# A two-layer hybrid trunk on one core: partition changes in four transfers instead of sixteen, keys ahead of queries, small steps spread out

## The chip, the cores and the metric

The kernel runs on one core of a Trainium2 chip. The metric is the device time of one execution in microseconds (us), lower is better. TensorE (PE in the profile) multiplies matrices, VectorE (DVE) and ScalarE (ACT) work on tiles, GpSimd (POOL) does small work and issues transfers, SyncE (SP) issues transfers.

## The reference

A sequence of 256 tokens of width 2048 goes through two layers. Each projects the normalised input once and gives the columns to three mixers, whose gated outputs are merged and added to x:

```python
def hybrid_layer(x, ...):
    h = rms_norm(x, norm_g)
    (c_q, c_kv, k_rope, z_a, u_b, v_b, z_b, q_c, k_c, v_c, a_r, z_c, gate_logits) = split(h @ w_in)
    y_a = mla_branch(c_q, c_kv, k_rope, ...) * silu(z_a)
    y_b = sgu_branch(gelu(u_b), gelu(v_b), ...) * silu(z_b)
    y_c = gla_branch(q_c, k_c, v_c, a_r, ...) * silu(z_c)
    g = sigmoid(gate_logits)
    merged = sum(g[b] * (y[b] @ w_branch[b]) for b in range(3))
    return x + merged @ w_out

def mla_branch(c_q, c_kv, k_rope, ...):          # 8 heads, 128 plain + 64 rotary
    q = rms_norm(c_q) @ w_uq
    k_nope, v = rms_norm(c_kv) @ w_ukv
    q, k = rms_norm(q), rms_norm(concat(k_nope, k_rope))   # per head; then the rotary part is turned
    return causal_block_attention(q, k, v)       # blocks of 128 queries
```

The sgu mixer multiplies by a 128 x 128 position matrix per group; the gla mixer is a gated linear attention with a decay from a_r, in chunks of 128.

## The kernel before

**Products.** All is float32. Each operand of a big product is split in a high part and a rest (`whi`, `wlo` of the weights; two halves of `xT`, `cT`, `mT`, `yT`), and three products of 128 x 512 make one. `Weights.chunk` loads 512 KB of weights (`wraw`, 4 buffers, queue SP), ACT copies `whi` (L65) and DVE subtracts `wlo` (L66), 3 buffers each. `block` (L194) goes over the chunks; a chunk is 12 products on PE (L207 to L209: two slices of the contraction, two token tiles, three products). So 24 products are a block of 4 slices, as those on `cT` are. The tokens' side has to stand with its features on the partitions.

**Small work.** Everything else is handed out in steps. After every three products `block` calls `step()`, which draws one step from the first generator in the list `work`; `pause(n)` lets n steps pass. `finish()` draws what is left. The framework's scheduler then sets each engine's order, with the weight splits ahead, and puts in the waits. Engines run their instructions in that order, so whoever stands behind a wait waits too.

**Changing partitions.** `move` (L269) brings features to the partitions: DVE transposes blocks of 32 x 32 into `part` (L275), and 16 transfers of 32 KB, in runs of 128 bytes, carry `part` to its place (L282). `move_split` (L284) moves into `whole` and splits that in two with ACT (L229) and DVE (L230). For the last groups (`mT3`, and `xT2`, `xT3` of the next layer) `transpose_split` (L246) has PE transpose with the identity (L242, tile `ptr`) instead.

**A layer**, in the order of PE: the two low-rank inputs `cq` (moved to `cT`, queue POOL), a narrow block of 96 columns (`accT`: the shared rotary key `krT`, the decay's input `arT`), the gate `sza`, then seven blocks on `cT`: queries (three: two plain, one rotary), keys (two, `kn`), values (two). The decay's products `pk` and `pz` (`decay`, L410) come 44 steps after they are put on the list. Queries and keys go through squares, sums and `r_q`, `r_k` on POOL (L126), rotation on DVE, and `move`: `qTn`, `qTr`, `kTz`, `kTn`. Meanwhile PE goes on with the `qc` block; the scores (`psc`, L561 and L563), the transposed probabilities (`ppt`) and the values (`ppv`) are drawn between its products. Then the gla mixer (`plv`, factors `X`, `AT`), the sgu mixer, the merge (`mT`) and the output (`xT`).

Of the kernel before, what the change touches and what calls it, by code (L numbers as in the profile page):

```python
# [71 lines left out]
def trunk(ctx: ExitStack, tc: tile.TileContext, a, out):  # L72
# [49 lines left out]
    def rsqrt(ss, n, inv, name):  # L122
        m = ts(f"m_{name}")
        V.tensor_scalar(m[:, :n], ss, inv, EPS, ALU.mult, ALU.add)
# [51 lines left out]
    work, pending = [], set()  # L176
# [13 lines left out]
    def finish():  # L190
        while work:
            step()
# [44 lines left out]
    def transpose2(src, b):  # L237

        p = pB("ptr")
        for k in range(2):  # L240
            for t in range(NT):
                nc.tensor.transpose(p[:, k * S + t * P:k * S + (t + 1) * P],  # L242
                                    src[:, t, (b + k) * P:(b + k + 1) * P], ident)
        return p

    def transpose_split(src, scale, name):  # L246

        dst = t8(name, F32R)
        pending.add(id(dst))
        dv = dst.rearrange("p (h k s) -> p h (k s)", h=2, k=4)  # L250

        def steps():
            yield from pause(4)
            ps = [transpose2(src, kk) for kk in (0, 2)]
            for kk, p in zip((0, 2), ps):
                if callable(scale):
                    for k in range(2):
                        c = slice((kk + k) * S, (kk + k + 1) * S)
                        split(dv[:, 0, c], dv[:, 1, c], p[:, k * S:(k + 1) * S], scale(kk + k))
                else:  # L260
                    c = slice(kk * S, (kk + 2) * S)
                    split(dv[:, 0, c], dv[:, 1, c], p, scale)
            pending.discard(id(dst))
            yield

        work.append(steps())
        return dst

    def move(dst, src, queue=nc.sync):  # L269

        part = t4("part")
        for t in range(NT):
            V.transpose(part.rearrange("p (k t c) -> p k t c", k=4, t=NT)[:, :, t, :],  # L275
                        src[:, t, :].rearrange("p (k c) -> p k c", k=4))
        pv = part.rearrange("p (n i b) -> p n i b", n=8, i=4)
        dst = dst if isinstance(dst, list) else [dst, dst]
        dv = [d.rearrange("p (n j b) -> p n j b", n=8, j=4) for d in dst]
        for j in range(4):  # L280
            for i in range(4):
                queue.dma_start(dv[i // 2][32 * i:32 * i + 32, :, j, :], pv[32 * j:32 * j + 32, :, i, :])  # L282

    def move_split(src, scale, name, queue=nc.sync, wait=0):  # L284

        dst, whole = t8(name, F32R), t4("whole")
        dv = dst.rearrange("p (h n) -> p h n", h=2)
# [3 lines left out]
        def steps():  # L291
            yield from pause(wait)
            if callable(scale):
                for k in range(4):
                    c = slice(k * S, (k + 1) * S)
                    split(dv[:, 0, c], dv[:, 1, c], whole[:, c], scale(k))
            else:
                split(dv[:, 0], dv[:, 1], whole, scale)
            pending.discard(id(dst))
            yield  # L300

        if wait:
            work.append(steps())
        else:
            list(steps())
# [40 lines left out]
    for l in range(DEPTH):  # L346
# [63 lines left out]
        def decay():  # L410
# [9 lines left out]
            for t in range(NT):  # L420
# [8 lines left out]
                V.scalar_tensor_tensor(la[:, t, :], z, 0.0, e, ALU.min, ALU.subtract)  # L429
# [22 lines left out]
        def rotate(dst, tmp, src, j, shape):  # L452
# [3 lines left out]
            V.tensor_tensor(dst, src, bc(TA, 0, 64), ALU.mult)  # L456
            V.tensor_tensor(tmp[:, :, :, 0:32], src[:, :, :, 32:64], bc(TB, 0, 32), ALU.mult)
            V.tensor_tensor(tmp[:, :, :, 32:64], src[:, :, :, 0:32], bc(TB, 32, 32), ALU.mult)
            V.tensor_tensor(dst, dst, tmp, ALU.add)

        def squares(dst, src):

            for t in range(NT):
                sq = t4("sq")[:, 0:src.shape[2]]
                act(sq, src[:, t, :], AF.Square)
                V.tensor_reduce(dst[:, t * 8:(t + 1) * 8], sq.rearrange("p (h d) -> p h d", h=NH), AX.X, ALU.add)

        qkg = ts("qkg", 1)
        V.tensor_tensor(qkg, gain(l, 24), gain(l, 25), ALU.mult)
        qn = t8("qn").rearrange("p (t c) -> p t c", t=NT)  # L470
        qr = t4("qr").rearrange("p (t c) -> p t c", t=NT)
        qTn = t8("qTn")
        for j in range(3):
            acc = block(lq, 4)
            for t in range(NT):
                dst = qn[:, t, j * 512:(j + 1) * 512] if j < 2 else qr[:, t, :]
                act(dst, acc[t], AF.Copy, scale=rc[:, t:t + 1])
        ssq = ts("ssq", 32)
        squares(ssq[:, 0:16], qn)
        squares(ssq[:, 16:32], qr)  # L480
        V.tensor_tensor(ssq[:, 0:16], ssq[:, 0:16], ssq[:, 16:32], ALU.add)
        rq = rsqrt(ssq[:, 0:16], 16, 1.0 / 192, "q")
        rqs = ts("rqs")
        V.tensor_scalar(rqs, rq, SCALE, None, ALU.mult)
        qrr, qrt = t4("qrr"), t4("qrt")
        rotate(v4(qrr), v4(qrt), qr.rearrange("p t (h d) -> p t h d", h=NH), 0, NH)
        qTr = t4("qTr")

        def half(dst, src, j):
            move(dst[:, j * 1024:(j + 1) * 1024], src[:, :, j * 512:(j + 1) * 512], nc.gpsimd)  # L490

        def move_queries():
            half(qTn, qn, 0)
            yield from pause(14)
            move(qTr, qrr.rearrange("p (t c) -> p t c", t=NT), nc.gpsimd)
            yield from pause(14)

        work.append(move_queries())
# [4 lines left out]
        kn = t8("kn").rearrange("p (t c) -> p t c", t=NT)  # L503
        for j in range(2):
            acc = block(lk, 4)
            for t in range(NT):
                act(kn[:, t, j * 512:(j + 1) * 512], acc[t], AF.Copy, scale=rc[:, 2 + t:3 + t])
        ssk = ts("ssk")
        squares(ssk[:, 0:16], kn)
        for t in range(NT):  # L510
            V.tensor_scalar(ssk[:, t * 8:(t + 1) * 8], ssk[:, t * 8:(t + 1) * 8], sskr[:, t:t + 1], None, ALU.add)
        rk = rsqrt(ssk[:, 0:16], 16, 1.0 / 192, "k")
        rk4 = rk.rearrange("p (t h) -> p t h", t=NT)
        krs = t4("krs")
        V.tensor_tensor(v4(krs), v1(krr).broadcast_to([P, NT, NH, 64]),
                        rk4.unsqueeze(3).broadcast_to([P, NT, NH, 64]), ALU.mult)
# [6 lines left out]
        kf = kn.rearrange("p t (h d) -> p (t h) d", h=NH)  # L523
        V.tensor_tensor(kf, kf, rk.unsqueeze(2).broadcast_to([P, 16, P]), ALU.mult)
        kTn = t8("kTn")

        def move_keys():
            move(kTz, krs.rearrange("p (t c) -> p t c", t=NT), nc.gpsimd)
            yield from pause(14)
            half(kTn, kn, 0)  # L530
            yield from pause(14)
            half(qTn, qn, 1)
            yield from pause(14)
# [429 lines left out]
```

## Time and profile before

| | us |
|---|---|
| median of three runs | 1860.86 |
| lowest and highest | 1855.51, 1862.33 |
| the profiled execution, own time | 1858.54 |
| its span | 1856.8 |
| PE busy in it | 1832.8 (99%) |
| DVE, ACT, POOL busy | 1131.2, 918.5, 188.1 |

The profiled execution is one that the hardware profiler recorded; its span is the time from its first to its last instruction, 1.7 us shorter than its own time. A product's start is exact, while its end is modelled, so a row's duration overlaps the next row's. All times of the prediction are set against 1858.54.

### The profile page before, as it was taken

The page shows a single profiled execution, that of the slowest core. Times are in us where ns is not written, and L with a number is a line of the kernel's source. Part 1 is how long each engine was busy: PE and PEld are TensorE (multiplying, and loading weights), DVE is VectorE, ACT ScalarE, POOL GpSimd, SP SyncE. Part 2 cuts the span into 40 slices and gives each one's busy share as a digit, 9 for nine tenths or more (in the row PEclk, how much of TensorE's full clock was granted, in tenths as well). Part 3 has the DMA queues.
Part 4 walks back from the last instruction along what each step waited for, and adds up shares of the span by engine and source line. Part 5 has one row for each costly group of instructions (what it writes and reads, how often), then busy time and mean ns, then how long its engine had stood idle before and what let it go on. Part 6 is the DMA issues. An engine that isn't in the chain of part 4 may idle for free.

```text
span 1856.8 us, 22945 instructions
## 1 busy us (share of the span) xinstructions
PE 1832.8 (99%) x8312; PEld 1518.6 (82%) x8312; DVE 1131.2 (61%) x1450; ACT 918.5 (49%) x1124; POOL 188.1 (10%) x301
## 2 busy tenths in 40 slices
PE   8999999999999999999999999999999999999999
PEld 7877888888888888888888778888888888888887
DVE  6766657876455655555566656578664556454554
ACT  6764445564444344444456635455544444444443
POOL 2217500000000000000022274000000000000000
PEclk9999999999999999999999999999999999999999
DMA  9657775475566665666866588754755766656754
GB/s 318 219 182 207 185 223 182 144 213 185 193 208 201 204 205 193 206 203 217 255 210 195 190 204 189 219 182 151 212 182 193 211 200 205 205 192 208 239 198 158
DMA packets 211026, 375.24 MB, mean 202 GB/s; under 512 B 119776, under 2 KB 120448, under 8 KB 210400
## 3 DMA queue, kind: packets, MB, share of 16 engines
q1 hardware_dynamic: 198624, 352.60, 60.3%
q0 software_dynamic: 10848, 18.78, 3.9%
q10 hardware_dynamic: 1440, 2.39, 0.4%
q8 instruction: 65, 1.06, 0.2%
q14 instruction: 49, 0.40, 0.1%
HBM read 348.52 MB, written 4.19 MB: 190 GB/s over the span
## 4 chain that ended last, share of the span: by engine, by line
PE 78%; DMA 2%; DVE 1%; POOL 1%; issue 1%; ACT 0%; SPq 0%; DVEq 0%; ACTq 0%; POOLq 0%
PE acc L209 25%; PE acc L207 25%; PE acc L208 25%; PE plv L706 1%; DMA kTn<-part 1%; DMA kTz<-part 1%; PE po L729 0%; PE pmx L803 0%; DVE wlo L66 0%; DMA qTn<-part 0%; DMA qTr<-part 0%; PE psc L563 0%; PE ppv L594 0%; PE psc L561 0%; DMA whole<-part 0%
## 5 line engine op out<-in xcount | busy, mean ns | idle before, releaser
L66 DVE TENSOR_TENSOR wlo<-wraw,whi 128x1024 fp32r<-128x1024 f32 (+1 forms) x642 | 781.1, 1218 | 634.0 <-ACT whi L65 632.8
L65 ACT ACTIVATE whi<-wraw 128x1024 fp32r<-128x1024 f32 (+1 forms) x642 | 677.3, 1056 | 792.9 <-PE acc L209 745.2
L207 PE MATMUL acc<-whi,xT 128*128 128x512 f32 x1792 | 703.1, 393 | 8.7 <-ACT whi L65 8.7
L208 PE MATMUL acc<-wlo,xT 128*128 128x512 f32 x1792 | 701.1, 391 | 5.2 <-DVE wlo L66 5.2
L209 PE MATMUL acc<-whi,xT 128*128 128x512 f32 x1792 | 700.6, 391 | 0.0
L207 PEld LDWEIGHTS acc<-whi,xT 128*128 128x128 f32 x1792 | 337.8, 189 | 78.5 <-ACT whi L65 9.5
L208 PEld LDWEIGHTS acc<-wlo,xT 128*128 128x128 f32 x1792 | 338.0, 189 | 75.8 <-DVE wlo L66 6.9
L209 PEld LDWEIGHTS acc<-whi,xT 128*128 128x128 f32 x1792 | 337.9, 189 | 70.0
L207 PE MATMUL acc<-whi,mT 128*128 128x512 f32 x256 | 99.9, 390 | 0.0
L209 PE MATMUL acc<-whi,mT 128*128 128x512 f32 x256 | 99.8, 390 | 0.0
L208 PE MATMUL acc<-wlo,mT 128*128 128x512 f32 x256 | 99.6, 389 | 0.0
L209 PEld LDWEIGHTS acc<-whi,mT 128*128 128x128 f32 x256 | 48.1, 188 | 9.9
L207 PEld LDWEIGHTS acc<-whi,mT 128*128 128x128 f32 x256 | 48.1, 188 | 9.9
L208 PEld LDWEIGHTS acc<-wlo,mT 128*128 128x128 f32 x256 | 48.1, 188 | 9.9
L207 PE MATMUL acc<-whi,yTa 128*128 128x512 f32 x128 | 49.8, 389 | 0.0
L208 PE MATMUL acc<-wlo,yTa 128*128 128x512 f32 x128 | 49.8, 389 | 0.0
L209 PE MATMUL acc<-whi,yTa 128*128 128x512 f32 x128 | 49.8, 389 | 0.0
L207 PE MATMUL acc<-whi,yTb 128*128 128x512 f32 x128 | 49.8, 389 | 0.0
L208 PE MATMUL acc<-wlo,yTb 128*128 128x512 f32 x128 | 49.8, 389 | 0.0
L209 PE MATMUL acc<-whi,yTb 128*128 128x512 f32 x128 | 49.8, 389 | 0.0
L207 PE MATMUL acc<-whi,yTc 128*128 128x512 f32 x128 | 49.8, 389 | 0.0
L208 PE MATMUL acc<-wlo,yTc 128*128 128x512 f32 x128 | 49.8, 389 | 0.0
(235 smaller groups left out, 1551.9 us busy)
## 6 DMA issues: line engine op xcount, KB each, us to landing
wraw<-in_w_big SPq DMA_DIRECT2D x634, 512.0 KB, 4.3
whole<-part SPq DMA_DIRECT2D x320, 32.0 KB, 4.2
x<-x POOLq DMA_DIRECT2D x8, 512.0 KB, 4.7
x<-in_x SPq DMA_DIRECT2D x2, 1024.0 KB, 8.9
whole<-part POOLq DMA_DIRECT2D x64, 32.0 KB, 4.1
qTn<-part POOLq DMA_DIRECT2D x64, 32.0 KB, 4.8
kTn<-part POOLq DMA_DIRECT2D x64, 32.0 KB, 5.2
qkT<-part SPq DMA_DIRECT2D x64, 32.0 KB, 4.1
```

The costliest lines, as they stand in the source:

```text
L65: nc.scalar.activation(hi[:, c], raw[:, c], AF.Copy)
L66: nc.vector.tensor_tensor(lo[:, c], raw[:, c], hi[:, c].bitcast(F32), ALU.subtract)
L207: nc.tensor.matmul(o, xh[:, c], wh, start=kt + k == 0, stop=False)
L208: nc.tensor.matmul(o, xh[:, c], wl, start=False, stop=False)
L209: nc.tensor.matmul(o, xl[:, c], wh, start=False, stop=kt + k == kts - 1)
L706: nc.tensor.matmul(p[:, h * P:(h + 1) * P], X[:, 0, h, :], X[:, 1, h, :], start=True, stop=True)
```

## The change

1. `move` orders `part` otherwise: the transposes read every fourth column (16 bytes apart) and 4 transfers of 128 KB, in runs of 1 KB, carry it (8 of 64 KB for `kTz`, which has two halves). What lands is in the order "j n b" and `natural` reads it back in order: in ACT's and DVE's splits, in an added copy by ACT (`qTn`, `qTr`, `qkT`), or directly in the score products.
2. The splits are cut in 4 or 8 pieces and come by a timer, `after(n, f)`, n steps later, instead of at once or from the list.
3. `transpose_split` is gone: `mT3`, `xT2`, `xT3` use `move_split` with a wait of 12 steps. The decay's generator so comes earlier, as the splits of `cT` don't stand ahead of it on the list.
4. Keys are projected ahead of queries (also in the weights' order, `_lay_out`); their movement is one generator, each query half has its own, and the rotation and the squares are spread over steps. The factor SCALE is put into `r_q`'s power.

```diff
 def rsqrt(ss, n, inv, name, times=1.0):
...
+    def after(n, f):
+        timers.append((clock[0] + n, f))
     def step():
+        clock[0] += 1
+        for t in [t for t in timers if t[0] <= clock[0]]:
+            timers.remove(t)
+            t[1]()
...
-    def transpose2(src, b):
...
-    def transpose_split(src, scale, name):
...
+    def natural(d):
+        return d.rearrange("p (j n b) -> p n j b", j=4, n=8)
     def move(dst, src, queue=nc.sync):
         part = t4("part")
         for t in range(NT):
-            V.transpose(part.rearrange("p (k t c) -> p k t c", k=4, t=NT)[:, :, t, :],
-                        src[:, t, :].rearrange("p (k c) -> p k c", k=4))
...
-        for j in range(4):
-            for i in range(4):
-                queue.dma_start(dv[i // 2][32 * i:32 * i + 32, :, j, :], pv[32 * j:32 * j + 32, :, i, :])
+            V.transpose(part.rearrange("p (i k t b) -> p t k i b", i=4, k=4, t=NT)[:, t],
+                        src[:, t, :].rearrange("p (k b i) -> p k i b", k=4, i=4))
+        dst = dst if isinstance(dst, list) else [dst]
+        for j in range(4):
+            o = slice(j * 256, (j + 1) * 256)
+            pv = part[32 * j:32 * j + 32, :].rearrange("p (i n) -> p i n", i=4)
+            for k, d in enumerate(dst):
+                r = slice(64 * k, 64 * k + 64) if len(dst) == 2 else slice(0, 128)
+                queue.dma_start(d[r, o], pv[16 * k:16 * k + 16] if len(dst) == 2 else pv)
     def move_split(src, scale, name, queue=nc.sync, wait=0):
...
+        def parts():
             if callable(scale):
+                for n in range(8):
+                    split(dv[:, 0, n], dv[:, 1, n], wv[:, n], scale(n // 2))
             else:
+                for j in range(4):
+                    split(dv[:, 0, :, j], dv[:, 1, :, j], wv[:, :, j], scale)
             pending.discard(id(dst))
+        after(wait, parts)
...
+        def keys():
+            yield from pause(4)
+            krs = rotary_keys()
+            yield from pause(1)
             move(kTz, krs.rearrange("p (t c) -> p t c", t=NT), nc.gpsimd)
+            for j in range(2):
+                yield from pause(4)
+                kf = heads(kn, j).rearrange("p t (h d) -> p t h d", h=4)
+                V.tensor_tensor(kf, kf, th(rk, j).unsqueeze(3).broadcast_to([P, NT, 4, P]), ALU.mult)
+                yield
+                move(half(kTn, j), heads(kn, j), nc.gpsimd)
+        work.append(keys())
+        def move_queries(j):
+            yield from pause(4)
+            whole = t4("whole")
+            move(whole, heads(qn, j), nc.gpsimd)
+            after(14, lambda: act(pieces(half(qTn, j)), natural(whole), AF.Copy, scale=qkg))
...
+        def rotary_queries():
+            yield from pause(2)
+            qrr, qrt = t4("qrr"), t4("qrt")
+            yield from rotate_steps(v4(qrr), v4(qrt), qr.rearrange("p t (h d) -> p t h d", h=NH), 0, NH)
+            whole = t4("whole")
+            move(whole, qrr.rearrange("p (t c) -> p t c", t=NT), nc.gpsimd)
             yield from pause(14)
+            act(pieces(qTr), natural(whole), AF.Copy)
+            yield from pause(2)
...
-        mT.append(transpose_split(merge_block(3), 0.5, "mT3"))
+        mT.append(move_split(merge_block(3), 0.5, "mT3", wait=12))
...
-                turn = move_split if nb < 2 else transpose_split
-                xT.append(turn(x, lambda k, l=l, nb=nb: gain(l + 1, 4 * nb + k), f"xT{nb}"))
+                xT.append(move_split(x, lambda k, l=l, nb=nb: gain(l + 1, 4 * nb + k), f"xT{nb}", wait=12))
```

**ACT behind the narrow block of layer 0.** Before, `arT` is copied, the weights' splits go on, and the splits of the second low-rank input (`cT_523`) and the decay's key (`kr`, from the tile `pk`) come later:

```order
L399 ACTIVATE arT<-accT 32x256 x2
L65 ACTIVATE whi<-wraw 128x1024 x4
L229 ACTIVATE cT_523<-whole,first_in 128x256 x2
L404 ACTIVATE wa<-wa_raw 96x512
L65 ACTIVATE whi<-wraw 128x1024
L229 ACTIVATE cT_523<-whole,first_in 128x256 x2
L65 ACTIVATE whi<-wraw 128x1024 x2
L440 ACT_TABLE_LOAD
L440 ACTIVATE th<-acc_659,rs 128x512
L65 ACTIVATE whi<-wraw 128x1024
L440 ACTIVATE th<-acc_660,rs 128x512
L417 ACTIVATE junk,sskr<-pk,r_x 128x64
```

After (`cT_511` is that second input):

```order
L376 ACTIVATE arT<-accT 32x256 x2
L237 ACTIVATE cT_511<-whole,first_in 128x128 x4
L65 ACTIVATE whi<-wraw 128x1024
L237 ACTIVATE cT_511<-whole,first_in 128x128 x4
L381 ACTIVATE wa<-wa_raw 96x512
L65 ACTIVATE whi<-wraw 128x1024
L394 ACTIVATE junk,sskr<-pk,r_x 128x64
L395 ACTIVATE kr<-pk,r_x 128x64
L237 ACTIVATE cT_502<-whole,first_in 128x128 x2
L394 ACTIVATE junk,sskr<-pk,r_x 128x64
```

The splits of `cT_511` moved ahead of four weight splits, and `pk`'s readers ahead of the gate's `th`.

**PE at the first scores of layer 0.** Before, one of the scores' groups is followed by eight products of the `qc` block (`acc`):

```order
L563 MATMUL psc<-kTn,qTn 128x128
L208 MATMUL acc_1840<-wlo,xT_94 128x512
L209 MATMUL acc_1840<-whi,xT_94 128x512
L207 MATMUL acc_1839<-whi,xT_94 128x512
L208 MATMUL acc_1839<-wlo,xT_94 128x512
L209 MATMUL acc_1839<-whi,xT_94 128x512
L207 MATMUL acc_1840<-whi,xT_94 128x512
L208 MATMUL acc_1840<-wlo,xT_94 128x512
L209 MATMUL acc_1840<-whi,xT_94 128x512
L584 MATMUL ppt<-c_ident,smx 128x128
```

After:

```order
L552 MATMUL psc<-kTn,qTn 128x128
L216 MATMUL acc_1405<-wlo,xT_96 128x512
L217 MATMUL acc_1405<-whi,xT_96 128x512
L215 MATMUL acc_1404<-whi,xT_97 128x512
L574 MATMUL ppt<-c_ident,smx 128x128
L550 MATMUL psc<-kTz_1106,qTr 128x256
L574 MATMUL ppt<-c_ident,smx 128x128
L552 MATMUL psc<-kTn,qTn 128x256
```

Three products stand there now. The scores themselves moved later in the block (slices `xT_96` where it was `xT_94`).

**POOL in layer 0 from the query's reciprocal root on.** Before, `r_k` stands behind the 32 transfers of `qTn` and `qTr`:

```order
L126 TENSOR_TENSOR r_q<-m_q,neghalf 128x16
L282 DMA qTn<-part 32x8x32 x16
L282 DMA qTr<-part 32x8x32 x16
L126 TENSOR_TENSOR r_k<-m_k,neghalf 128x16
L521 MEMSET kTz_1298 64x1024
L522 MEMSET kTz_1299 64x1024
```

After, the keys' end, the queries' and the rotary queries' transfers (the three `whole`):

```order
L263 DMA kTz_1107<-part 64x1x256
L263 DMA kTn<-part 128x1x256 x8
L263 DMA whole<-part 128x1x256 x8
L126 TENSOR_TENSOR r_q<-m_q,neghalf 128x16
L263 DMA whole<-part 128x1x256 x4
```

`r_k` moved ahead of all of these (and of eight transfers of `kTz`), and `r_q` to just ahead of the rotary queries.

## Rows read from the trace of the kernel before

**Rows 1.** The profile's first part: busy time, share of the span and instructions of each engine:

```profile
PE 1832.8 (99%) x8312; PEld 1518.6 (82%) x8312; DVE 1131.2 (61%) x1450; ACT 918.5 (49%) x1124; POOL 188.1 (10%) x301
```

**Rows 2.** The waits of PE: line, what it waited for, time in total, times, longest, in us (longest row):

```profile
PE acc L207 <- ACT whi L65: 8.7, 3, 5.6
```

**Rows 3.** Timeline of PE in layer 0, 131 to 199 us: start, duration, engine, line, operation, output<-inputs, and in brackets the idle time ahead of it with what ended it:

```profile
131.63 0.50 PE L207 MATMUL acc<-whi,cT 128*128 128x512 f32 x1 [1.72 <-ACT kn L507]
...
156.17 0.49 PE L207 MATMUL acc<-whi,xT 128*128 128x512 f32 x1 [2.48 <-ACT whi L65]
157.43 0.50 PE L208 MATMUL acc<-wlo,xT 128*128 128x512 f32 x1 [0.77 <-DVE wlo L66]
...
158.56 0.63 PE L209 MATMUL acc<-whi,xT 128*128 128x512 f32 x1
...
161.12 0.63 PE L209 MATMUL acc<-whi,xT 128*128 128x512 f32 x1
...
167.95 0.50 PE L208 MATMUL acc<-wlo,xT 128*128 128x512 f32 x1 [0.46 <-DVE wlo L66]
...
198.35 0.35 PE L563 MATMUL psc<-kTn,qTn 128*128 128x128 f32 x1 [1.68 <-issue]
```

**Rows 4.** The same timeline of PE in layer 1, 1054 to 1122 us:

```profile
1054.92 0.50 PE L207 MATMUL acc<-whi,cT 128*128 128x512 f32 x1 [1.72 <-ACT kn L507]
...
1077.63 0.51 PE L207 MATMUL acc<-whi,xT 128*128 128x512 f32 x1 [0.65 <-ACT whi L65]
1078.89 0.51 PE L208 MATMUL acc<-wlo,xT 128*128 128x512 f32 x1 [0.76 <-DVE wlo L66]
...
1090.53 0.79 PE L208 MATMUL acc<-wlo,xT 128*128 128x512 f32 x1 [3.18 <-DVE wlo L66]
...
1121.15 0.46 PE L563 MATMUL psc<-kTn,qTn 128*128 128x128 f32 x2 [0.51 <-DMA kTn<-part]
```

**Rows 5.** Timelines of ACT and of POOL in layer 0, the row of each at 154 and 160 us:

```profile
154.02 1.15 ACT L538 ACTIVATE qTn<-qTn,qkg 128x1024 f32<-128x1024 f32 x1 [7.07 <-DMA qTr<-part]
...
160.37 2.94 POOL L126 TENSOR_TENSOR r_k<-m_k,neghalf 128x16 f32<-128x16 f32 x1
```

**Rows 6.** Timeline of PE where eight transposes of x stand, and two products behind them:

```profile
911.52 1.04 PE L242 MATMUL ptr<-c_ident,x 128*128 128x128 f32 x8
912.32 0.47 PE L207 MATMUL acc<-whi,mT 128*128 128x512 f32 x1
912.63 0.39 PE L208 MATMUL acc<-wlo,mT 128*128 128x512 f32 x1
```

**Rows 7.** Timeline of PE at the first products behind the narrow block, in layer 0 (two) and in layer 1:

```profile
57.65 0.40 PE L207 MATMUL acc<-whi,xT 128*128 128x512 f32 x1
57.88 0.40 PE L208 MATMUL acc<-wlo,xT 128*128 128x512 f32 x1
...
980.94 0.40 PE L207 MATMUL acc<-whi,xT 128*128 128x512 f32 x1
```

**Rows 8.** Timeline of POOL in layer 0 at 57 us and in layer 1 at 980 us:

```profile
57.48 1.04 POOL L126 TENSOR_TENSOR r_c<-m_c,neghalf 128x4 f32<-128x4 f32 x1 [9.39 <-DVE m_c L124]
58.48 8.11 POOL L282 DMA_DIRECT2D whole<-part  x14
...
979.54 6.38 POOL L282 DMA_DIRECT2D whole<-part  x11
```

**Rows 9.** The profile's part on DMA issues: output<-input, issuing engine, count, KB of each, median us from issue to landing:

```profile
wraw<-in_w_big SPq DMA_DIRECT2D x634, 512.0 KB, 4.3
...
whole<-part POOLq DMA_DIRECT2D x64, 32.0 KB, 4.1
...
kTn<-part POOLq DMA_DIRECT2D x64, 32.0 KB, 5.2
...
rope_g<-in_rope_g ACTq DMA_DIRECT2D x1, 128.0 KB, 2.8
```

**Rows 10.** Instructions grouped by line and shape: count | busy us, mean ns of one | idle time of the engine ahead of them:

```profile
L66 DVE TENSOR_TENSOR wlo<-wraw,whi 128x1024 fp32r<-128x1024 f32 x634 | 774.5, 1223 | 631.6 <-ACT whi L65 630.5
L65 ACT ACTIVATE whi<-wraw 128x1024 fp32r<-128x1024 f32 x634 | 671.4, 1060 | 788.9 <-PE acc L209 741.6 <-issue 28.4 <-DVE wlo L66 5.0
...
L574 ACT ACTIVATE smx<-smx,nbias,rqs 128x128 f32<-128x128 f32 x16 | 7.7, 482 | 10.9 <-DVE nbias L572 10.9
...
L229 ACT ACTIVATE cT<-whole,first_in 128x256 fp32r<-128x256 f32 x16 | 7.2, 500 | 3.5 <-DMA whole<-part 2.2 <-DMA ba<-in_b_a 1.3
...
L126 POOL TENSOR_TENSOR r_k<-m_k,neghalf 128x16 f32<-128x16 f32 x2 | 5.9, 2934 | 0.0
...
L538 ACT ACTIVATE qTn<-qTn,qkg 128x1024 f32<-128x1024 f32 x4 | 4.6, 1144 | 12.3 <-DMA qTr<-part 7.1 <-DMA qTn<-part 5.2
...
L275 DVE STREAM_TRANSPOSE part<-qrr 128x512 f32<-128x512 f32 x4 | 2.5, 666 | 0.0
...
L418 ACT ACTIVATE kr<-pk,r_x 128x64 f32<-128x64 f32 x4 | 1.2, 304 | 0.0
```

**Rows 11.** Timeline of DVE in the gated linear attention of layer 0: one step of the factors and the masked copies of two levels:

```profile
331.27 0.44 DVE L715 COPY_PREDICATED AT<-c_lvl,plv 128x256 f32<-128x256 int32 x1
...
352.56 0.42 DVE L694 TENSOR_TENSOR X<-X,qkT 128x256 f32<-128x256 f32 x1
352.89 1.31 DVE L715 COPY_PREDICATED AT<-c_lvl,plv 128x256 f32<-128x256 int32 x2
```

More of the change, by code (lines that the diff above doesn't have):

```diff
@@ L190, in finish @@
     def finish():
-        while work:
+        while work or timers:
             step()
@@ new lines, in trunk @@
+        rotate(v1(krr), v1(krt), v1(kr), 1, 1)
+        kn = t8("kn").rearrange("p (t c) -> p t c", t=NT)
+        ssk = ts("ssk")
+        for j in range(2):
+            acc = block(lk, 4)
+            for t in range(NT):
+                act(heads(kn, j)[:, t], acc[t], AF.Copy, scale=rc[:, 2 + t:3 + t])
+            squares(th(ssk[:, 0:16], j), heads(kn, j), 4)
+        for t in range(NT):
+            V.tensor_scalar(ssk[:, t * 8:(t + 1) * 8], ssk[:, t * 8:(t + 1) * 8], sskr[:, t:t + 1], None, ALU.add)
@@ L470, in trunk @@
+        rk = rsqrt(ssk[:, 0:16], 16, 1.0 / 192, "k")
+        kTz = [t4("kTz0"), t4("kTz1")]
+        nc.gpsimd.memset(kTz[0][64:128, :], 0.0)
+        nc.gpsimd.memset(kTz[1][0:64, :], 0.0)
+        kTn = t8("kTn")
         qn = t8("qn").rearrange("p (t c) -> p t c", t=NT)
         qr = t4("qr").rearrange("p (t c) -> p t c", t=NT)
-        qTn = t8("qTn")
+        qTn, qTr = t8("qTn"), t4("qTr")
+        pieces = lambda v: v.rearrange("p (n j b) -> p n j b", n=8, j=4)
+        half = lambda v, j: v[:, j * 1024:(j + 1) * 1024]
@@ L486, in trunk @@
[L486 to L493, printed above, removed]
-            yield from pause(14)
-            move(qTr, qrr.rearrange("p (t c) -> p t c", t=NT), nc.gpsimd)
-            yield from pause(14)
-        work.append(move_queries())
-        krr, krt = ts("krr", 128, 1), ts("krt", 128, 1)
@@ L502, in trunk @@
-        rotate(v1(krr), v1(krt), v1(kr), 1, 1)
[L503 to L511, printed above, removed]
@@ L525, in trunk @@
[L525 to L533, printed above, removed]
-            half(kTn, kn, 1)
-            yield from pause(14)
-            for j in range(2):
-                c = slice(j * 1024, (j + 1) * 1024)
-                act(qTn[:, c], qTn[:, c], AF.Copy, scale=qkg)
-            yield from pause(4)
@@ L634, in trunk @@
         for j in range(2):
-            move(qkT[:, j], qk[:, j])
+            whole = t4("whole")
+            move(whole, qk[:, j])
+            after(14, lambda j=j, w=whole: act(pieces(qkT[:, j]), natural(w), AF.Copy))
         vc = t8("vc").rearrange("p (t c) -> p t c", t=NT)
@@ L643, in trunk @@
         finish()
-        yT = {0: [move_split(ya[:, :, j * 512:(j + 1) * 512], 0.5, f"yTa{j}") for j in range(2)]}
+        yT = {0: [move_split(ya[:, :, j * 512:(j + 1) * 512], 0.5, f"yTa{j}", wait=14) for j in range(2)]}
         AT = t4("AT")
@@ L843, in trunk @@
         finish()
-        yT[1] = [move_split(uz[:, :, j * 512:(j + 1) * 512], 1.0, f"yTb{j}") for j in range(2)]
+        yT[1] = [move_split(uz[:, :, j * 512:(j + 1) * 512], 1.0, f"yTb{j}", wait=14) for j in range(2)]
         gate_block(1)
         for nb in range(2):
-            mT.append(move_split(merge_block(nb), 0.5, f"mT{nb}"))
+            mT.append(move_split(merge_block(nb), 0.5, f"mT{nb}", wait=14))
         gate_block(2)
```

116 lines of the change are left out of this document (42 added, 74 removed).

## The prediction

> **What bounds the kernel now.** The profile's first part comes first: PE is busy for 1832.8 of 1856.8 us [rows 1], so only 24 us are idle, and what isn't idle is product after product at a fixed spacing: behind the narrow block they start 0.23 us apart [rows 7], 24 of them (one block on `cT`) in 5.44 us. The time can fall in two ways, by fewer PE instructions or by fewer waits of PE. So the waits of PE come next: most are for the weights' split on ACT [rows 2]. That doesn't make ACT the limit; the timeline of PE shows where these waits lie: nearly all in the attention, between the blocks on `cT` and the first scores, once in each layer [rows 3, 4].
>
> In layer 0 the idle times there are 1.72, 2.48, 0.77, 0.46 and 1.68 us, 7.1 together; each hides 0.16 more, as a row's modelled 0.39 is longer than the spacing of 0.23: 7.9. Behind the wait at 156 us seven products run 0.43 apart ((161.12 - 158.56)/6) instead of 0.23, another 1.4 [rows 3]. Layer 1 has 1.72, 0.65, 0.76, 3.18 and 0.51, 6.8, with the hidden part 7.6, and I take as long a slow stretch behind its longest wait, 1.4 [rows 4]. Together 18.3 us.
>
> The cause is a queue. ACT sat 7.07 us at the copy of `qTn`, for transfers of `qTr`, with weights' splits queued behind it; and POOL reached `r_k` only at 160.37 us, behind all the queries' transfers, so the keys came late too [rows 5]. A transfer costs POOL 8.11/14 = 0.58 us to issue, and a move has 16, thus 9.3 us [rows 8].
>
> **The change, part by part.**
>
> *Transposes on PE go.* There are 32. Eight hold the products up from 911.52 to 912.63 less one spacing, 0.88 us [rows 6]; four times that is 3.5 us off PE for certain. In their place `mT3`, `xT2` and `xT3` take four DVE transposes (0.67 each [rows 10]), four issues, a landing and pieces of splits: some 12 us. PE comes to that slice after 12 slices of 6 products, 16.3 us. It holds, but on DVE and ACT the splits stand between weights' splits, which leaves by the order as little as 0.4 us. I cost it at nothing.
>
> *The old waits go.* With four transfers a move takes POOL 2.3 us instead of 9.3, `r_k` stands ahead of all of these, and the copy of `qTn` no longer waits behind the rotary queries. The 18.3 us go, if nothing takes their place. Three things do.
>
> *How long a move takes to land (L).* No row shows a transfer of 128 KB from SBUF to SBUF in runs of 1 KB. The nearest are `rope_g`, 128 KB in 1-KB runs, 2.8 us, and the old moves, 4.1 to 5.2, which are as long as a weight load of 512 KB, 4.3 [rows 9]. The bounds are 2.8 and 5.2; I take 3.4, nearer the row of the same size and runs, as that one ran on another queue. The page "DMA: Bandwidth & Descriptors" of the Trainium skill (section "Why small descriptors are slow (HBM only)") says that transfers within SBUF don't suffer from small runs; by that rule 1-KB runs land no sooner than 128-byte runs did, and the sum would be that of the first rival.
>
> *New wait at the decay.* `pk` comes 15 products behind the narrow block, its second half 17 further on, and that waits for ACT's `kr`. ACT now has the splits of `cT_511` ahead of it, and these wait for the move. Layer 0: `r_c` ends at 58.5, four issues end at 60.8 [rows 8], landed at 60.8 + L. Then ACT does eight quarter splits (between 0.30 and 0.50 each, started some 0.1 closer: 0.28, 2.2 together), two weights' splits (2.1), `wa` and the readers of `pk` (about 1.2): 5.5 us [rows 10]. So 66.3 + L, with L = 3.4 at 69.7. PE is there at 57.65 + 32 x 0.227 and a little, 65.2 [rows 7]: it waits 4.5 us. Behind that wait are weights' splits too, so PE has nothing else. Layer 1: POOL is free at 979.5, landed at 981.9 + L, ACT done at 990.8; PE, from 980.94, comes at 988.3: 2.5 us. Together 7.0, and a slow stretch behind the longer wait, 1.4. At L = 2.8 it is 5.8, at 5.2 it is 10.6, with the stretch besides.
>
> *New wait ahead of the scores.* Times from the first product on `cT`. Keys end at 10.9, their `r_k` (2.93 [rows 10]) at about 16.5, the rotary keys are turned and moved from about 22; then eight issues for `kTz`, eight for `kTn`, eight for `whole` of the queries: the last issue at about 39.5, with DVE's transposes between (an estimate from 0.58 an issue and 0.67 a transpose). DVE's rotation of `qr` needs a buffer that this move frees, 39.5 + L; its rest, four transposes and two or three weights' subtractions (1.22 each) and four issues take 9.1, another L, and the added copy to `qTr` 1.14 like `qTn`'s [rows 10]: 49.7 + 2L = 56.5. PE comes to the first score after 168 products on `cT` and 70 of `qc`, 54.0, with half a us of small waits 54.5. It waits 2.0 us in each layer, 4.0 in all. At L = 2.8 it is 1.6, at 5.2 it is 11.2 in all.
>
> *Fewer products between scores.* Eight scores, then three products (0.7 us) to the first `ppt`; before there were eight (1.8 us). From score to `ppt` lie the masked maxima on DVE and the exponent on ACT (0.48 [rows 10]), 1.5 to 2 us; later groups have `ppt` and `ppv` without any products. Upper bound 3.2 us a layer; lower bound nothing, as smaller waits stand there now. I take 2.0, in two layers 4.0.
>
> *What costs nothing.* SP issues 4 instead of 16 transfers a move; no PE wait lies there. Three copies of 1.14 on ACT a layer, hidden: ACT is 49% busy [rows 1]. The products between the levels of the gla mixer are spread otherwise (15 each); DVE's eight factor steps of 0.42 and two masked copies a level [rows 11] run ahead of that by a few us, by the order, so at most 1 us is lost or won. The transposes read every fourth column. Rows bound what that can do: the factor step 352.56, at a level that reads in scattered short runs, takes 0.42 as at every level, while the masked copies take 1.31/2 = 0.65 there and 0.44 at a coarser level [rows 11]. So between nothing and half as much again (0.3 us each); I take nothing, as the transpose has one input like the factor step rather than the copy's three.
>
> *Sum.* -18.3 - 3.5 + 7.0 + 1.4 + 4.0 + 4.0 = -5.4. From the profiled execution's 1858.5 (2.3 below the median of the three) that gives **1853**. L = 2.8 gives 1849.5, L = 4.2 gives 1858.
>
> **The rivals.**
>
> *1. Moves land as slowly as now.* L = 4.2 to 5.2. For it: the old moves land with the weight loads, 4.1 to 5.2 against 4.3, as if they queued together [rows 9]. Against it: fewer and larger pieces, and `rope_g`. At 5.2: -21.8 + 10.6 + 1.4 + 11.2 + 4.0 = +5.4. 1858 to 1864.
>
> *2. The new waits are covered.* L near 2.8 or below, pauses that overlap what I laid end to end, and scores that cost no more than now. What stays is the decay's wait in layer 0, 4 us: 1858.5 - 21.8 + 4 = 1841. For it: a chain laid out by hand is an upper bound wherever a DVE or ACT step can slip ahead. Against it: in layer 0 `pk` waits for a chain that nothing can shorten.
>
> *3. The strided transposes are slow.* This ends slower. If each takes twice its 0.67, a move takes 2.7 us longer. The second half of `cT` has it in its chain in both layers (5.4), the rotary queries too (5.4), the two `mT3` and `xT3` have little slack (2 to 2.5 each, 7 in all); 18 us: 1871, with some hidden 1868. Each 0.1 us of a transpose is worth 2.6; from 0.2 on the change gives nothing, from 0.55 on it is slower by 0.5%. Against it: the factor step's 0.42; for it: the masked copy's 0.65 [rows 11]. The page "SBUF — State Buffer" of the Trainium skill (its note on cachelines, section "Door 1") says that lines are of 16 bytes and each step to a new line costs; by that rule every element of these transposes, 16 bytes apart, would pay. The masked copy agrees, the factor step doesn't.
>
> **How the numbers follow.** A difference under 0.5%, 9.3 us, can't be told from none here. My forecast 0.38, rival 1 0.13, rival 2 0.34, rival 3 0.15. Faster than 1849.2: rival 2 and 0.06 of the forecast, 0.40. Slower: 0.12 of rival 3 and 0.03 of rival 1, 0.15. The rest, 0.45, is the same. The likeliest's own range is 1849 to 1858; with the others 1839 to 1866, which leaves out part of rivals 2 and 3, under 0.2.
>
> **What the profile after would show.** No `ptr` on PE and 32 instructions fewer. The waits of PE at `acc` for ACT's `kn` gone; no ACT idle of 7 us at `qTn`. A PE idle of 3 to 6 us within 10 us behind the narrow block of layer 0, ended by ACT (`kr` or a weights' split), about half in layer 1. The first score waits 1 to 3 us for the `qTr` copy. The moves' landing between 2.8 and 4.2 in the DMA part, and the transposes at 0.67 still. It is wrong if transposes take 0.9 or more, if the landing is outside, or if waits appear in the gla mixer or at `mT3`.

## The result and the profile after

The changed kernel takes 1880.8 us (median; 1879.2 to 1881.4) against 1861.3 of the kernel before: a ratio of 1.011, 95% interval 1.0088 to 1.0132. The forecast was 1853, with a range up to 1866. It is 20 us slower, where I had it 5 faster.

The page's first part, to compare with [rows 1]:

```profile
PE 1837.6 (98%) x8280; PEld 1519.7 (81%) x8280; DVE 1179.2 (63%) x1560; ACT 938.8 (50%) x1232; POOL 81.7 (4%) x117
```

PE has 32 instructions fewer (8280 for 8312), and the span is 1879.1 instead of 1856.8 us: of the 22.3 us more, 17.5 are idle PE (41.5 us instead of 24.0) and the rest is busy time that runs slowly. POOL fell from 188 to 82 us, and DVE rose by 48.

The waits of PE (engine, line, what it waited for, us in total, times, longest; [rows 2] has the longest row of before):

```profile
PE psc L550 <- issue: 12.6, 2, 6.5
PE acc L216 <- DVE wlo L66: 9.7, 13, 1.3
PE acc L215 <- ACT whi L65: 5.8, 2, 5.6
PE pk L392 <- ACT kr L395: 4.4, 1, 4.4
PE pz L400 <- DVE wa L382: 3.7, 1, 3.7
```

The names have changed. Waits for whi in the attention are gone (the 5.6 here is at the start of the kernel); waits for the first scores (`psc`), for `wlo`, and at `pk` and `pz` have come. The timeline of PE, as in [rows 3, 4] (start, duration, output<-inputs, idle time ahead of it and what ended it); the row at 1002 us is of layer 1:

```profile
69.22 0.37 PE L392 MATMUL pk<-c_ident,krT 64*128 64x64 f32 x1 [4.38 <-ACT kr L395]
70.11 0.63 PE L215 MATMUL acc<-whi,xT 128*128 128x512 f32 x1
70.54 0.63 PE L216 MATMUL acc<-wlo,xT 128*128 128x512 f32 x1
...
139.71 0.50 PE L216 MATMUL acc<-wlo,cT 128*128 128x512 f32 x1 [1.25 <-DVE wlo L66]
...
148.36 0.50 PE L216 MATMUL acc<-wlo,cT 128*128 128x512 f32 x1 [1.11 <-DVE wlo L66]
...
177.11 0.76 PE L550 MATMUL psc<-kTz,qTr 128*128 128x128 f32 x2 [6.16 <-issue]
...
1002.58 0.49 PE L400 MATMUL pz<-wa,arT 96*128 96x512 f32 x1 [3.67 <-DVE wa L382]
```

Here are the new waits of layer 0: 4.38 us at `pk`, where before nothing stood still, 1.25 and 1.11 for `wlo` between the blocks on `cT`, and 6.16 at the first score. Behind `pk` products run 0.43 us apart (70.11 to 70.54) instead of 0.23. Three stretches of layer 0, behind the wait at `pk`, a little later, and behind the wait at the first score (length; busy us of PE, PEld, DVE, ACT and POOL, each with its instructions; then the granted clock as a share of full speed, the DMA share and GB/s):

```profile
69.50:74.40 4.90, 4.90 (x13) 3.82 (x13) 4.00 (x8) 3.56 (x11) 0.00 (x0) 0.50 0.34 128
75.00:80.00 5.00, 5.00 (x23) 4.10 (x23) 3.28 (x9) 3.56 (x5) 0.00 (x0) 1.00 0.34 114
177.20:180.50 3.30, 3.30 (x16) 3.30 (x17) 0.67 (x5) 0.50 (x3) 0.00 (x0) 0.50 0.00 0
```

After each of the two long waits PE is granted the lower of its two levels, 0.50 (1.2 GHz), for 3 to 5 us, and then the full one. So the first scores, 16 products of 128 columns, started 0.21 apart instead of 0.11 and took 3.4 us instead of 1.8.

### The profile page after: what moved, and what is told of

The parts are those of the page before. It is cut to its first block, busy times and chain, and to the rows that moved or that the text cites. A ratio compares the mean times of both kernels' runs of the same rounds, so it can differ in the third digit from the quotient of the medians.

```text
span 1879.1 us, 22545 instructions
## 1 busy us (share of the span) xinstructions
PE 1837.6 (98%) x8280; PEld 1519.7 (81%) x8280; DVE 1179.2 (63%) x1560; ACT 938.8 (50%) x1232; POOL 81.7 (4%) x117
## 3 DMA queue, kind: packets, MB, share of 16 engines
q8 instruction: 65, 1.06, 0.2%
## 4 chain that ended last, share of the span: by engine, by line
PE 86%; issue 4%; DVE 4%; DMA 3%; ACT 2%; POOL 1%; SPq 0%; ACTq 0%; DVEq 0%; POOLq 0%
PE acc L216 27%; PE acc L217 27%; PE acc L215 27%; DMA whole<-part 2%; DVE wlo L66 2%; DMA wraw<-in_w_big 2%; DVE part L255 1%; ACT whi L65 1%; PE plv L698 1%; PE psc L550 1%; PE psc L552 1%; PE ppv L584 1%; POOL whole L263 0%; POOL r_k L126 0%; PE po L721 0%
## 5 line engine op out<-in xcount | busy, mean ns | idle before, releaser
L65 ACT ACTIVATE whi<-wraw 128x1024 fp32r<-128x1024 f32 (+1 forms) x642 | 675.8, 1054 | 711.9 <-PE acc L217 667.5
L216 PE MATMUL acc<-wlo,cT 128*128 128x512 f32 x112 | 44.5, 398 | 6.0 <-DVE wlo L66 5.8
## 6 DMA issues: line engine op xcount, KB each, us to landing
wsT<-in_w_sT POOLq DMA_DIRECT2D x2, 1024.0 KB, 10.4
```

What stands on the lines that cost most here:

```text
L65: nc.scalar.activation(hi[:, c], raw[:, c], AF.Copy)
L216: nc.tensor.matmul(o, xh[:, c], wl, start=False, stop=False)
```

## Experiments

The price of each cause is the difference from the changed kernel's ratio of 1.011, 1% being 18.6 us. Ratios and not times are subtracted, as the kernel before was timed again beside each group of runs and its median moved between 1860.9 and 1863.3 us. Each ratio's interval reaches 2 to 5 us either way, so a price is known to some 5 us.

**1. Contiguous transposes.** The columns of the weights, and of x, are laid out so that column 32i + b of each 128 holds what was column 4b + i. Then a transpose's block is contiguous and its output the same as before; only the two rotary moves still read every fourth column. The result is turned back outside the measured time, as x is turned ahead of it.

```diff
-                        src[:, t, :].rearrange("p (k b i) -> p k i b", k=4, i=4))
+                        src[:, t, :].rearrange("p (k b i) -> p k i b" if apart else "p (k i b) -> p k i b", k=4, i=4))
...
+    def turned(w):
+        n = w.shape[-1]
+        return w.reshape(w.shape[:-1] + (n // P, 32, 4)).swapaxes(-1, -2).reshape(w.shape)
```

> The changed kernel, with the columns of the weights (and of x) laid out in the order that lets the transposes read contiguous blocks of 32; only the two rotary moves (krs, qrr) still read every fourth column. The rest is the changed kernel. Theory A (the strided transposes, 1.08 us instead of 0.67, stretch the DVE chains): transposes at 0.67 to 0.71, PE's waits for wlo fall from 9.7 us to under 3, the waits at the first scores from 12.6 to about 6, pk's from 4.4 to about 3; 11 to 14 us less than the changed kernel, 1867 to 1870. Theory B (the landing of the moves, 4.0 to 4.9 us, sets the waits): the score waits stay over 10 us and the time stays over 1875.

Measured: 1874.5 us, ratio 1.0067 (1.0046 to 1.0089), 8 us less than the changed kernel. Transposes in this run, `kn` contiguous and `qrr` strided (count, busy us, mean ns, idle):

```profile
L255 DVE STREAM_TRANSPOSE part<-kn 128x512 f32<-128x512 f32 x8 | 5.2, 695 | 0.0
...
L255 DVE STREAM_TRANSPOSE part<-qrr 128x512 f32<-128x512 f32 x4 | 4.1, 1071 | 0.0
```

and its waits of PE:

```profile
PE psc L550 <- issue: 12.3, 2, 6.2
...
PE acc L216 <- DVE wlo L66: 3.5, 7, 0.8
```

The same instruction on the same amount of data takes 0.70 us contiguous and 1.07 at a step of 16 bytes. The stride costs; the waits for `wlo` fell from 9.7 to 3.5. But half of my expectation missed: the waits at the first scores stayed at 12.3. Both sides of that wait came earlier, PE by about 3 us as it lost less on the way, and the rotary queries by as much. So 8 us and not 11 to 14, at 1874.5 instead of 1867 to 1870, and neither theory was whole.

**2. The decay at 44 steps.**

```diff
         def decay():
-            yield from pause(4)
+            yield from pause(44)
```

> The changed kernel with the decay's products (pk, pz) 44 steps behind the narrow block instead of 4. Theory A (PE stands at pk and pz for ACT and DVE work that is queued behind the splits of cT): the waits of 4.4 and 3.7 us go and with them the slow stretches behind them, 9 to 11 us less than the changed kernel, 1870 to 1872. Rival: the weights' splits stand behind the same splits of cT, so the wait only moves to acc, 3 to 4 us at each place, and the time stays within 4 us of the changed kernel's 1881.

Measured: 1873.3 us, ratio 1.0063 (1.0039 to 1.0088), 8.7 us less than the changed kernel. The waits at `pk` and `pz` are gone. In their place PE's timeline has, in layer 0 and 1:

```profile
66.15 0.49 PE L215 MATMUL acc<-whi,xT 128*128 128x512 f32 x1 [0.89 <-ACT whi L65]
67.41 0.50 PE L216 MATMUL acc<-wlo,xT 128*128 128x512 f32 x1 [0.77 <-DVE wlo L66]
...
996.33 0.49 PE L215 MATMUL acc<-whi,xT 128*128 128x512 f32 x1 [0.59 <-ACT whi L65]
997.59 0.50 PE L216 MATMUL acc<-wlo,xT 128*128 128x512 f32 x1 [0.77 <-DVE wlo L66]
```

This is the rival's wait, but 1.4 to 1.7 us, not 3 to 4: the weights' splits do stand behind the splits of `cT`, and I take it that PE has weights in hand that cover most of it. Theory A held, with a gain a little under its 9 to 11.

**3. Both.**

> Both edits, contiguous transposes and the decay at 44 steps. If the two causes are separate, their gains add: 20 to 25 us less than the changed kernel, 1856 to 1861, about the kernel before. If one covers the other, no more than the larger of them, 1867 or above.

Measured: 1864.1 us, ratio 1.0011 (0.9996 to 1.0025), 18.4 us less than the changed kernel; 8.0 and 8.7 make 16.7. The sum expected, 20 to 25, was missed because each gain was; the two causes add, as far as the intervals tell. The kernel now equals the one before. Its waits at the first scores were still 11.6 us.

**4. Queries first.** The queries' three blocks and the keys' two change places in the changed kernel.

> The changed kernel with the queries' three blocks ahead of the keys' two again (their weights too). If the keys' place ahead is what costs (their moves stand ahead of the queries' on POOL and DVE), the first scores wait less than 6 us instead of 12.6 and the time falls to 1874 or below. If the strided transposes and the landing cost it, the keys' sixteen transfers now come last and the score waits grow to 14 to 20 us, 1883 to 1890.

Measured: 1875.1 us, ratio 1.0076 (1.0052 to 1.01), 6 us less than the changed kernel, and the waits of PE are others:

```profile
PE acc L215 <- ACT whi L65: 11.6, 4, 5.9
PE acc L216 <- DVE wlo L66: 5.7, 10, 1.3
...
PE psc L551 <- DMA kTn<-part: 3.5, 2, 1.8
PE psc L549 <- DMA kTn<-part: 1.2, 2, 0.7
```

The scores wait 4.7 us instead of 12.6, now for `kTn`. Waits for whi rise to 11.6 (5.9 of it at the start), as ACT again stands, 7.30 us at `qTr` in layer 0, with weights queued behind it. The waits went as the first case has it, and the time missed its 1874 by 1 us. So in the changed kernel keys ahead of queries cost some 6 us, though the two intervals overlap; the eighth run has the order once more.

**5. The scores later.** On top of the third run, the copy to `qTr`, and with it everything behind, waits 44 steps. The first score stands 35 places later on PE.

```diff
-            yield from pause(14)
+            yield from pause(44)
             act(pieces(qTr), natural(whole), AF.Copy)
```

> The kernel with contiguous transposes and the decay at 44 steps, and with the copy to qTr and the scores behind it 44 instead of 14 steps after the rotary queries' move (the first score stands 30 to 35 products later on PE). Theory C (PE waits 6 us at the first score because the program puts that score ahead of the time at which the rotary queries land, not because anything is slower): the waits at the first scores (11.6 us) and the slow stretch behind them go; 12 to 16 us less than without this edit, 1848 to 1852. Rival D (ACT stands 6 us at the copy to qTr, with weights' splits behind it, as before the change at qTn): the wait moves to acc for ACT's whi, 2 to 5 us a layer remain, 1854 to 1860.

Measured: 1856.1 us, ratio 0.9972 (0.9957 to 0.9987), 7.3 us less than the third run: rival D's range. The waits at scores are gone. The timelines of ACT and of PE show what is left:

```profile
167.81 1.06 ACT L527 ACTIVATE qTr<-whole 128x1024 f32<-128x1024 f32 x1 [6.19 <-DMA whole<-part]
...
169.86 0.50 PE L215 MATMUL acc<-whi,xT 128*128 128x512 f32 x1 [1.16 <-ACT whi L65]
171.12 0.50 PE L216 MATMUL acc<-wlo,xT 128*128 128x512 f32 x1 [0.76 <-DVE wlo L66]
```

ACT's place for the copy did not move: the same two weights' splits stand ahead of it as in the third run. Why the scheduler left it there no run shows. ACT stood 6.19 us for the transfers, two weights' splits waited behind it, and PE stood 1.16 and 0.76 us for these.

**6. The copy on POOL.**

```diff
-            act(pieces(qTr), natural(whole), AF.Copy)
+            nc.gpsimd.tensor_copy(pieces(qTr), natural(whole))
```

> As the run with the later scores, but the copy to qTr is made by POOL, so that no weights' split stands behind it. Theory C: the same time as that run, within 2 us. Rival D: 3 to 8 us less than that run, 1847 to 1851. By both the kernel is faster than the one before (1861) by 0.5% or more.

Measured: **1850.1 us, ratio 0.994 (0.9917 to 0.9963)**, 6 us less than the fifth run; fifth and sixth edits together 13 us. The copy takes 1.52 us on POOL, where nothing is behind it:

```profile
167.46 1.52 POOL L527 COPY qTr<-whole 128x1024 f32<-128x1024 f32 x1 [5.45 <-DMA whole<-part]
```

```profile
PE acc L215 <- ACT whi L65: 5.9, 2, 5.6
PE acc L216 <- DVE wlo L66: 5.2, 9, 0.8
PE acc L215 <- ACT qr L511: 1.1, 2, 0.6
```

Theory C gave the 13 us, rival D gave how they split. Of PE's waits the 5.6 at the start remains, and pieces of 0.15 to 0.76 for `wlo`. This kernel beats both.

**7. Runs of 128 bytes.** The third run's kernel, its four transfers writing straight into the natural order in runs of 128 bytes.

```diff
-        return d.rearrange("p (j n b) -> p n j b", j=4, n=8)
+        return d.rearrange("p (n j b) -> p n j b", j=4, n=8)
...
-            pv = part[32 * j:32 * j + 32, :].rearrange("p (i n) -> p i n", i=4)
+            pv = part[32 * j:32 * j + 32, :].rearrange("p (i n b) -> p i n b", i=4, n=8)
```

> The kernel with contiguous transposes and the decay at 44 steps (measured at 1864), its four transfers writing runs of 128 bytes instead of 1 KB, straight into the natural order, so that only the size of the runs differs. Theory B1 (runs of 128 bytes cost the transfers): the landing of whole on POOL goes from 5.3 to 7 us or more, the waits at the first scores grow by 3 us or more each, 1870 or above. Theory B2 (the landing is set by the weight loads in flight, not by the runs): landing within 0.5 us of 5.3, the time within 3 us of 1864.

Measured: 1895.9 us, ratio 1.0183 (1.0159 to 1.0207), 32 us more than the third run. DMA part (KB of each, us to landing) and two waits of PE:

```profile
whole<-part SPq DMA_DIRECT2D x112, 128.0 KB, 4.8
...
whole<-part POOLq DMA_DIRECT2D x40, 128.0 KB, 7.6
...
kTn<-part POOLq DMA_DIRECT2D x16, 128.0 KB, 7.9
```

```profile
PE psc L549 <- issue: 18.2, 2, 9.2
PE acc L215 <- ACT qr L510: 14.2, 2, 7.5
```

On POOL's queue the landing goes to 7.6 us, from 5.3 in the third run; on SP's only from 4.5 to 4.8. At the same bytes and the same count of transfers, short runs do land later, and theory B1 holds. POOL itself is also held longer: issuing one of these transfers takes it 0.89 us on average instead of 0.57. The waits grow more than the landing, as the chain holds several moves: `qr`'s eviction on ACT waits for a buffer that `kTn`'s transfers free, 7.5 us in layer 0, and the scores 9.2.

**8. Queries first, with the decay at 44 steps.** This was meant for the third run's kernel. The kernel that ran has the columns of the weights as in the changed kernel, so that its transposes are strided, as in the second run.

> The kernel with contiguous transposes and the decay at 44 steps, but queries' blocks ahead of keys'. If the order itself is worth something, this stands 4 us or more from the 1864 of the same kernel with keys first: below, if the keys' transfers (waits of 1.8 us at kTn measured) are shorter than the 6 us at the first scores, 1856 to 1860; above, if ACT's stand at qTn (4 to 6 us) comes back in full, 1866 to 1870.

Measured: 1867.2 us, ratio 1.0032 (1.0017 to 1.0046). A transpose of this run, and its waits of PE:

```profile
L255 DVE STREAM_TRANSPOSE part<-merged 128x512 f32<-128x512 f32 x16 | 16.6, 1080 | 0.0
```

```profile
PE acc L215 <- ACT whi L65: 13.4, 6, 6.0
...
PE psc L549 <- DMA kTn<-part: 4.6, 2, 2.5
```

At 1.08 us a transpose, this run differs from the third in two things and says nothing on the cases expected. What it differs from in the order alone is the second run (1.0063): queries first take 5.8 us off it, as they took 6.3 off the changed kernel in the fourth. The scores wait 4.6 instead of 12.6 us, acc for whi 13.4 instead of 7.6. So keys ahead of queries cost some 6 us in both settings tried, each time at the edge of what the intervals tell apart. Whether they still do where the scores stand later no run tests.

**9. Only the scores' place.** The changed kernel with the edits of the fifth and sixth runs alone.

> The changed kernel (strided transposes, decay at 4 steps) with the first scores 44 instead of 14 steps behind the rotary queries' move and the copy to qTr on POOL. If the place of the first scores is a cause of its own: 12 to 16 us less than the changed kernel's 1881, 1865 to 1869, with the waits at the scores (12.6) gone and those at pk and pz (8.1) left. If the strided transposes push the rotary queries' landing behind the later scores too, 1 to 3 us of wait a layer stay there, 1869 to 1873.

Measured: 1866.8 us, ratio 1.0018 (1.0007 to 1.0029), 17 us less than the changed kernel by the ratios. That is the first case: its gain is a little over the 12 to 16, and the time lies in its range. It is the largest of the three causes, and it holds two edits: on the third run's kernel the later place gave 7.3 us and POOL's copy another 6. PE's waits at the scores are gone, those at `pk` and `pz` are 4.8 and 4.3.

**10. The stride with the others mended.**

> As the fastest kernel so far (1850), but with the strided transposes: decay at 44 steps, scores later, copy on POOL. What it has over 1850 is the price of the stride when nothing else stands in the way. If the three causes add, 6 to 9 us, 1856 to 1859, in waits for wlo (5 us there, about 10 here); if the stride only counted through the late scores, within 3 us of 1850.

Measured: 1859.9 us, ratio 0.9981 (0.9969 to 0.9992), 0.0041 or 7.6 us above the sixth run. So the stride costs as much here as in the first run, 8.0; neither price has the two rotary moves in it, which are strided in every run. The ninth run, which lacks only the decay's edit, is 6.9 us slower than this one, against the 8.7 of the second run. The stride's price lies, as expected, in waits for `wlo`, and in one that I hadn't named, `ppt` for ACT's exponents:

```profile
PE acc L216 <- DVE wlo L66: 10.6, 13, 1.2
...
PE ppt L574 <- ACT smx L564: 2.8, 3, 1.3
```

## Why the prediction was wrong, step by step

**Transposes off PE** and **the old waits gone** were right: no `ptr`, nothing waits at `kn` or `qTn`. But the kind of wait was not removed: ACT's stand of 7.07 us at `qTn` [rows 5] is one of 6.22 at `qTr`, below.

**The price of the strided transposes** failed first. A transpose, and `r_k`, as grouped rows of the changed kernel (`qrr`'s row is the same as in the first run):

```profile
L255 DVE STREAM_TRANSPOSE part<-kn 128x512 f32<-128x512 f32 x8 | 8.3, 1080 | 0.0
...
L126 POOL TENSOR_TENSOR r_k<-m_k,neghalf 128x16 f32<-128x16 f32 x2 | 7.6, 3776 | 125.3 <-DVE m_k L124 125.3
```

I took nothing, "as the transpose has one input like the factor step rather than the copy's three", and 0.3 as the upper bound. It is 0.4 (1.06 to 1.11 against 0.67 to 0.71), above the bound. The copy [rows 11] was the better neighbour in size. The factor step was none: by the program it reads every second column at its finest level, 8 bytes apart and so two elements of each 16 bytes, where the transposes read one. Rival 3's rate of 2.6 us for each 0.1 makes 10.4 of it, but it counts four transposes a move, where a move has two of 128 x 512 (the rows' counts: 4 of `qrr` for two layers); with two it makes 5.2. The runs say 8.0 and 7.6, and that without the rotary moves, which the rival counts in. So the rival was right in kind and within a factor of two in size; I gave it 0.15. The page "SBUF — State Buffer" of the Trainium skill (its note on cachelines, section "Door 1") says that accesses which each cross to a new line of 16 bytes pay. This instruction agrees, with 1.07 against 0.67 at a step of 16 bytes; no other step was tried.

**The landing** was mis-sized: 3.4 taken, measured

```profile
whole<-part SPq DMA_DIRECT2D x112, 128.0 KB, 4.0
...
whole<-part POOLq DMA_DIRECT2D x40, 128.0 KB, 4.9
...
kTn<-part POOLq DMA_DIRECT2D x16, 128.0 KB, 4.7
```

on POOL's queue 4.9 and 4.7. Rival 1 had it. The page "DMA: Bandwidth & Descriptors" of the Trainium skill (section "Why small descriptors are slow (HBM only)") says that transfers within SBUF don't suffer the penalty of small descriptors. The seventh run disagrees on POOL's queue, 7.6 us against 5.3. So the landing came out as by that rule, but not for its reason: the old transfers had shorter runs and also a quarter of the bytes, and how the two weigh no run separates.

**The wait at the decay** has the right mechanism, and its number in layer 0 is luck: 4.5 us forecast, 4.38 at `pk` measured. POOL's issues of the second `cT` input, and ACT's first splits of it:

```profile
55.85 2.24 POOL L263 DMA_DIRECT2D whole<-part  x4 [0.20 <-issue]
...
63.67 1.28 ACT L237 ACTIVATE cT<-whole,first_in 128x128 fp32r<-128x128 f32 x4 [4.76 <-DMA whole<-part]
```

From the end of the issues to the split it took 5.6 us where I had 3.4. But the issues ended 1.1 us behind the first product after the narrow block (56.99) where I had 3.2, taken over from the kernel before. The two misses, 2.2 and 2.1, cancel. In layer 1 the landing's miss stands alone (4.9 instead of 3.4), and the wait is 3.67 instead of 2.5; there `pz` waits for DVE's `wa` and not for `kr`. The slow stretch behind the wait was 1.4 in my sum, in one layer. It came in both: twelve products from 69.52 to 74.81 us took 2.6 us more than at 0.23 each, and in layer 1 it was about 2. So the trace has 8.05 of waits and 4.6 of slow stretches for my 7.0 and 1.4. The second run gives 8.7 of that back, as it keeps 1.7 and 1.4 us of waits at `acc`.

**The first scores** are where most went: 4.0 us taken, 12.6 measured, and 17 with all that hangs on it (ninth run). The chain in layer 0, rows of DVE, ACT and POOL:

```profile
156.89 1.23 DVE L433 TENSOR_TENSOR qrr<-qr,tabs 128x1024 f32<-128x1024 f32 x1 [2.19 <-DMA whole<-part]
165.36 2.07 DVE L255 STREAM_TRANSPOSE part<-qrr 128x512 f32<-128x512 f32 x2
...
175.96 1.06 ACT L527 ACTIVATE qTr<-whole 128x1024 f32<-128x1024 f32 x1 [6.22 <-DMA whole<-part]
...
124.96 3.77 POOL L126 TENSOR_TENSOR r_k<-m_k,neghalf 128x16 f32<-128x16 f32 x1 [63.79 <-DVE m_k L124]
...
152.69 2.17 POOL L263 DMA_DIRECT2D whole<-part  x4 [0.92 <-DVE part L255]
...
167.99 2.34 POOL L263 DMA_DIRECT2D whole<-part  x4 [0.91 <-DVE part L255]
```

The links, in us from the first product on `cT` (109.67 in PE's timeline):

| | forecast | measured |
|---|---|---|
| the queries' last issue ends | 39.5 | 45.2 |
| the rotation starts | 42.9 | 47.2 |
| the rotary queries' last issue ends | 52.0 | 60.7 |
| ACT's copy to `qTr` ends | 56.5 | 67.4 |
| PE comes to the first score | 54.5 | 61.3 |

The step that failed is this end-to-end chain, which I had called an upper bound. Up to the queries' last issue it was 5.7 short: `r_k` starts at 15.3, not 13.5, takes 3.77 instead of 2.93, and the ten strided transposes up to there cost 4.0 more. Then a landing of 3.4 came to 2.0, which gives back 1.4. The rotation and its move took 13.4 instead of 9.1: three of DVE's weights' splits (3.7), the rotation's four steps (3.8, of which I had about 1) and the squares' sums stand there, while the two transposes, at 2.07, are shorter than the four that I had counted. From the last issue to ACT's copy it took 5.6 rather than 3.4. PE itself came 6.8 later than forecast; 4.5 of these are waits, nearly all for `wlo`. So the data came 10.9 later, PE 6.8 later, and the wait is 4.1 longer. And I had no slow stretch behind this wait, which costs 1.6 us a layer (3.4 instead of 1.8 for 16 scores).

Yet the chain's length is not the cause of the loss by itself. The score's place on PE was. In the kernel before, the first product on `cT` and the first score of layer 0 stood here:

```profile
102.55 0.39 PE L207 MATMUL acc<-whi,cT 128*128 128x512 f32 x1
...
187.58 0.38 PE L561 MATMUL psc<-kTz,qTr 128*128 128x128 f32 x2
```

That is 85.0 us apart, with 171 products between the last one on `cT` and the score; in the changed kernel it is 70 products and 67.4 us, the wait included. So the data came earlier than the score's old place, but the score had moved up by 101 products, 23 us at 0.23 each, and that was too far. Where the change is described ahead of the prediction, I read the scores as having moved later in the block. That holds within a block only: the first score stands in the first block behind `cT`'s, where it had stood in the second. Why the scheduler chose that place no run shows. 35 products later no wait took its place, and there the same late data fit (ninth run). In my working that place stood as given.

**Fewer products between scores** was wrong in the other direction: 4.0 us taken, and PE's waits list no `ppt` in the changed kernel. With the scores later and the strided transposes it appears, 2.8 us in the ninth and tenth runs.

**What I costed at nothing** held mostly: no wait at `mT3` or `xT3`, and between the attention and the gla mixer one of 0.77 us in layer 0 and one of 0.51 in layer 1.

**The sum.** Three causes, each 8.0 (stride), 8.7 (decay) and 17.1 us (scores), make 33.8; all mended take 31.6 from the changed kernel, to 0.994. So they add, and they are what turned a forecast gain into a loss: of the three I had the stride at nothing, the scores at 4.0 and the decay at 8.4. What is left against the kernel before is a gain of 11 us, half of the 21.8 that I had released. The sixth run still has 6.3 us of waits for `wlo` and `qr`; the other 4 are as much as its interval. Which part earns the 11, the moves, the transposes taken off PE or the later places, no run separates, and the later places were not tried on the kernel before. The keys' place is no part of it as far as the runs go: queries first was faster both times.

## What to carry to other kernels

When a wait goes, look up what is next in the same queue and what its place in the program assumes: a tile that is ready too late for its place costs as much as a slow one, and moving the place was the cheapest remedy here. Compare that place with the one before the change, counted in products. A wait in the list is a difference between two times; shorten the work on both sides and it stays while the time falls. Price an instruction in a new access pattern by the worse of its neighbours, since a chain multiplies that price, and permuting the weights' columns may buy the pattern back without time on the chip, where input and result can be turned outside.

## What the runs showed of the hardware

- A 32 x 32 transpose of 128 x 512 on DVE: 0.67 to 0.71 us from contiguous blocks, 1.05 to 1.12 when it reads every fourth element, that is at 16 bytes (all runs).
- Transfers of 128 KB within SBUF, beside the weight loads: medians of 3.5 to 4.6 us to land on SP's queue and 4.4 to 5.4 on POOL's with runs of 1 KB (all runs but the seventh); 4.8 on SP's and 7.6 to 7.9 on POOL's with runs of 128 bytes (seventh run). Issuing one took POOL 0.56 to 0.61 us with runs of 1 KB and 0.89 with runs of 128 bytes.
- `r_k`, 16 powers on each of 128 partitions on POOL: 2.93 us in the kernel before [rows 10] and in the two runs with queries first, 3.77 to 3.78 in the changed kernel and the others, the same instruction on the same shape. What it shares the time with wasn't tested.
- After an idle time of 4.4 us, and after one of 6.2, in the changed kernel, PE's granted clock was the lower level, 0.50, for 3 to 5 us: products of 512 columns 0.43 us apart, scores of 128 columns 0.21.
